# A two-block network on one NeuronCore: elementwise work moved from GpSimd to VectorE, two modulation vectors summed on TensorE strips, and one tile for the rotation tables

## The chip, the cores and the metric

The kernel runs on one core of a Trainium2 chip. The metric is the time of one execution in microseconds on the device, the median of three runs. The engines are called TensorE (PE in the profile; PEld is its loading of weights), VectorE (DVE), ScalarE (ACT), GpSimd (POOL) and SyncE (SP, which here only issues DMAs).

## The reference

Two transformer-like blocks run one after the other on 256 tokens of width 2048, all in float32. What matters of them:

```python
# first block: six vectors of 2048 from the condition c modulate its two norms and gate its two halves
mod = silu(c) @ w_ada + b_ada                                  # 2048 x 12288
shift1, scale1, gate1, shift2, scale2, gate2 = split(mod, 6)   # parts 0 to 5
p = modulate(rms_norm(x), shift1, scale1) @ w_in               # fourier mix and a two-way mLSTM
x = x + gate1 * (mix @ w_out)
h2 = modulate(rms_norm(x), shift2, scale2)                     # the second norm: parts 3 and 4
a, v = split(conv(h2 @ w_up))
x = x + gate2 * ((silu(a) * v) @ w_down)
# second block: a gated FFN, a mixer of a diagonal state-space model (S5) and a sparse attention (NSA), a gated FFN
h = h + 0.5 * norm(swiglu(norm(h)))
proj = norm(h) @ w_in_2
x_t = a * x_{t-1} + b * u_t        # S5: 64 groups x 64 complex states
h = h + norm((sig(ga) * y_ssm + sig(gb) * y_nsa) @ w_out_2)
h = h + 0.5 * norm(swiglu(norm(h)))
```

## The kernel before

Activations lie feature by feature: a tile holds 128 features x 256 tokens. Every matrix is packed into **chunks** of 128 x 1024 floats (512 KB). Each chunk is loaded by SP into a raw tile `wr` (four buffers; while the first mixer runs, every third goes to one of two buffers `wa`). ScalarE copies it to `wh` (rounded to fp32r, three buffers), and raw minus `wh` gives the rest `wl` (two buffers); that subtraction, the **low part**, is VectorE's, except that in some stages every `pool_every`-th chunk's is GpSimd's (method `chunk`). TensorE then does three products of each weight tile, `wh` with the high and low half of the activation and `wl` with the high half: 24 matmuls of 128 x 128 x 256 a chunk. All linears go through `lin_steps`; their evacuations come from PSUM (eight banks `ps`) at the end of a group of output tiles.

Beside a linear, generators run as **background**: after each chunk every one in `self.bg` is advanced at a rate of its own. These matter here:

- `ada_part` makes a part of `mod` (parts 2, 4, 3 during the first mixer, part 5 during the up projection after it). It loads the 32 chunks of the part's matrix, and VectorE adds each, scaled by a column of `silu_c`, to an accumulator `acc` (a scalar_tensor_tensor of 128 x 1024). Sixteen one-column matmuls then sum over the partitions. Parts 0 and 1 are made otherwise, in `entry`, at the start: two matmuls a chunk with a stationary operand of 32 columns, each into its own quarter of the partitions of a bank (a **strip**). There `sil`, 32 columns a weight row with `silu_c` in the first and zeros in the others, is the stationary operand, and the four strips are summed with a column of ones.
- `s5_tables`, during the second block's first up projection (`up2`), builds for each of 32 state tiles a cosine and a sine table by complex products (`cmul`, six elementwise operations on GpSimd), and writes them to DRAM (`d_tab`).
- `s5`, during the projections `kv_in2`, `q_in2`, `gn_in2` and `ga_in2`, takes a state tile per step: two products of the input with the tables on VectorE, an add and a subtract on GpSimd, two scans (tensor_tensor_scan) on VectorE, two more products on VectorE, an add and a subtract on GpSimd. All its tiles are called `w`.
- `nsa`, from `ga_in2` on, is the attention.

GpSimd also multiplies the two halves of the gated FFNs (`hidden`), adds the first twelve squares for each norm (`add_square`), adds the residuals in `post_norm`, and takes some products and sums in the mixers. One line of the profile, L277, is `tt` on VectorE; L280 is `gtt`, the same on GpSimd; L283 is scalar_tensor_tensor on VectorE; L274 is ScalarE; L295 is every matmul.

The instructions of each engine stand in the order that the framework's scheduler finds from its own model of times; an engine works through its queue in that order.

Of the kernel before, what the change touches and what calls it, by code (L numbers as in the profile page):

```python
# [226 lines left out]
class Builder:  # L227
    def __init__(self, tc, ap, out):
        self.tc = tc
        self.nc = tc.nc  # L230
        self.ap = ap
        self.out = out
        self.n = 0
        self.bg = []
        self.nchunk = 0
        self.nraw = 0
        self.more = None
        self.pool_every = 0
# [40 lines left out]
    def gtt(self, out, a, b, op):  # L279
        return self.nc.gpsimd.tensor_tensor(out, a, b, op=op)  # L280

# [23 lines left out]
    def chunk(self, src, n):  # L305
# [89 lines left out]
    def add_square(self, st, src, scale=None):  # L395
# [9 lines left out]
        if n < 12:  # L405
            self.gtt(st["acc"], st["acc"], s, ALU.add)
# [68 lines left out]

    def modulated(self, xs, st, gain, shift):
# [16 lines left out]
    def setup(self):  # L493
# [9 lines left out]
        self.ones_col = self.ones[:, 0:1]  # L503
        self.eps = self.small("eps", [P, 1])
# [5 lines left out]
    def block1(self):  # L510
# [3 lines left out]
        with tc.tile_pool(name="mix1", bufs=1, reuse_waits="tile") as pm:  # L514
# [24 lines left out]
            self.pool_every = 0  # L539
# [53 lines left out]
    def hidden(self, ph, a, b):  # L593

        m = self.t2()
        self.gtt(m, a, b, ALU.mult)
# [6 lines left out]
    def entry(self, pm, M, xs, h):  # L603
# [17 lines left out]
        self.pool_every = 3  # L621
        stream = self.lin_steps("qk_in", act_h, ev_qk)

        sil = self.new(pm, "vh", [P, 2, T], F32, 7).rearrange("p a (b c) -> p (a b) c", c=32)
        nc.gpsimd.memset(sil, 0.0)
        nc.vector.tensor_copy(sil[:, :, 0:1], self.silu_c.unsqueeze(2))
# [7 lines left out]
        def sums(kp, qt):  # L634
# [6 lines left out]
            for i in range(2):  # L641

                rt = qt * 2 + i
                g = rt % 4 * 32
                self.mm(acc[g:g + 32], sil[:, rt], raw[:, i * 512:(i + 1) * 512], rt < 4, rt >= KD - 4, True)

        def total(kp):
            acc = self.t2().rearrange("p a b -> p (a b)")
            self.act(acc, accs.pop(kp), ACT.Copy)
            for e in range(4):  # L650
                c = 4 * kp + e
                self.mm(mods[:, 0, c:c + 1], acc[:, e * P:(e + 1) * P], self.ones_col, e == 0, True, True)
# [38 lines left out]
        self.pool_every = 2  # L691
# [3 lines left out]
    def mix1(self, pm, M, h, qk, graw):  # L695
# [79 lines left out]
        def ev_o(gi, banks):  # L775
            for _ in ml:
                pass
            for b in range(2):
# [3 lines left out]
                self.gtt(o, o, hm[hd], ALU.mult)  # L782
# [12 lines left out]
    def mlstm(self, pm, qk, vfm, graw, hm):  # L795
# [102 lines left out]
        def values(hd, d):  # L898
# [15 lines left out]
            else:  # L914
                self.gtt(hx, hx, held.pop(("h", hd)), ALU.add)
# [193 lines left out]
    def cmul(self, out_r, out_i, ar, ai, br, bi, u, v):  # L1109

        self.gtt(u, ar, br, ALU.mult)
        self.gtt(v, ai, bi, ALU.mult)
        self.gtt(out_r, u, v, ALU.subtract)
        self.gtt(u, ar, bi, ALU.mult)
        self.gtt(v, ai, br, ALU.mult)
        self.gtt(out_i, u, v, ALU.add)
# [563 lines left out]
```

## Time and profile before

| | us |
|---|---|
| median of 3 runs | 3678.48 (3677.97 to 3678.49) |
| the profiled execution | 3664.88 |
| its span, first to last instruction | 3662.9 |
| PE busy in the span | 3540.0 (97%) |
| DVE busy | 2178.8 (59%) |
| ACT busy | 1557.1 (43%) |
| POOL busy | 891.9 (24%) |

The numbers are those of one profiled execution. Busy is the time in which at least one instruction of the engine ran; a share over the whole span mixes stages with different limits. The profiled execution took 13.6 us less than the median of the runs.

### The profile page before, as it was taken

What the parts mean: (1) busy time and instruction counts of PE and PEld (TensorE: products, weight loads), DVE (VectorE), ACT (ScalarE), POOL (GpSimd) and SP (SyncE); (2) the same over time, 40 slices, a digit from 0 to 9 for tenths busy, and PEclk for the clock granted to TensorE, in tenths of its full rate; (3) what the DMA queues carried; (4) which work ended last, traced back from release to release, by engine and by line L of the source; (5) the groups of instructions that cost most, each with busy time, mean ns of one, the idle gap of its engine ahead of it and who ended that gap; (6) DMA issues with size and microseconds to landing.
All of it is one profiled execution on the core that took longest, in us unless ns stands there. A gap on an engine that the chain in (4) does not pass through costs nothing. (4 is left out here: it accounts for less than half of the span.)

```text
span 3662.9 us, 67909 instructions
## 1 busy us (share of the span) xinstructions
PE 3540.0 (97%) x28008; PEld 3386.3 (92%) x28008; DVE 2178.8 (59%) x2597; ACT 1557.1 (43%) x1996; POOL 891.9 (24%) x799
## 2 busy tenths in 40 slices
PE   7899999999999999999999899999999899999998
PEld 4688899999999998999999888888899899999997
DVE  2487766666554665655544689775535655555445
ACT  2343355454544443444434423345544444444333
POOL 1143510000011059910000246433232300000001
PEclk9899999999999999999999999999999899999999
DMA  9887857776555566665556455444455455555554
GB/s 341 292 298 260 296 180 229 222 229 201 184 185 183 164 196 201 214 202 183 182 183 184 151 166 170 157 142 125 121 179 182 137 184 184 182 183 183 185 184 139
DMA packets 213319, 710.82 MB, mean 194 GB/s; under 512 B 23904, under 2 KB 39296, under 8 KB 213008
## 3 DMA queue, kind: packets, MB, share of 16 engines
q1 hardware_dynamic: 213008, 706.48, 60.0%
q8 instruction: 219, 3.59, 0.4%
q14 instruction: 92, 0.75, 0.1%
HBM read 694.29 MB, written 11.57 MB: 193 GB/s over the span
## 5 line engine op out<-in xcount | busy, mean ns | idle before, releaser
L277 DVE TENSOR_TENSOR wl<-wr,wh 128x1024 fp32r<-128x1024 f32 x989 | 1285.8, 1302 | 1074.0 <-PE ps L295 984.4
L274 ACT ACTIVATE wh<-wr 128x1024 fp32r<-128x1024 f32 x1066 | 1127.8, 1058 | 1594.9 <-PE ps L295 1390.4
L295 PE MATMUL ps<-r,wh 128*128 128x256 f32 x12224 | 1767.8, 287 | 38.9 <-ACT r L274 22.8
L295 PEld LDWEIGHTS ps<-r,wh 128*128 128x128 f32 x12224 | 1605.8, 194 | 65.3 <-ACT r L274 28.3
L295 PE MATMUL ps<-r,wl 128*128 128x256 f32 x6112 | 1012.4, 288 | 33.3 <-DVE wl L277 29.5
L295 PEld LDWEIGHTS ps<-r,wl 128*128 128x128 f32 x6112 | 856.8, 195 | 59.1 <-DVE wl L277 38.6
L280 POOL TENSOR_TENSOR t<-t,t 128x512 f32<-128x512 f32 x66 | 104.2, 1579 | 1290.2 <-ACT t L274 946.4
L295 PE MATMUL ps<-hh,wl 128*128 128x256 f32 x2112 | 345.4, 283 | 0.0
L295 PE MATMUL ps<-hl,wh 128*128 128x256 f32 x2112 | 345.4, 283 | 0.0
L295 PE MATMUL ps<-hh,wh 128*128 128x256 f32 x2112 | 344.3, 283 | 0.0
L295 PEld LDWEIGHTS ps<-hl,wh 128*128 128x128 f32 x2112 | 293.9, 192 | 0.0
L295 PEld LDWEIGHTS ps<-hh,wl 128*128 128x128 f32 x2112 | 293.9, 192 | 0.0
L280 POOL TENSOR_TENSOR wl<-wr,wh 128x1024 fp32r<-128x1024 f32 x77 | 196.8, 2556 | 396.3 <-PE ps L295 300.0
L295 PEld LDWEIGHTS ps<-hh,wh 128*128 128x128 f32 x2112 | 293.2, 192 | 0.0
L280 POOL TENSOR_TENSOR acc<-acc,t 128x256 f32<-128x256 f32 x99 | 109.6, 1115 | 607.6 <-ACT t L274 604.3
L283 DVE SCALAR_TENSOR_TENSOR acc<-wr,silu_c,acc 128x1024 f32<-128x1024 f32 x89 | 128.4, 1443 | 53.2 <-DMA wr<-in_w_ada 52.8
L280 POOL TENSOR_TENSOR w<-w,w 128x256 f32<-128x256 f32 x128 | 125.1, 1003 | 127.3 <-DVE w L277 120.1
L295 PE MATMUL ps<-m,wh 128*128 128x256 f32 x1024 | 152.3, 287 | 0.0
L280 POOL TENSOR_TENSOR t<-hh,hh 128x256 f32<-128x256 f32 (+4 forms) x192 | 149.5, 806 | 2.6
L295 PEld LDWEIGHTS ps<-m,wh 128*128 128x128 f32 x1024 | 134.6, 193 | 3.6 <-ACT wh L274 0.3
L277 DVE TENSOR_TENSOR w<-ps,w 128x512 f32<-128x512 f32 (+1 forms) x96 | 58.7, 640 | 50.8 <-DMA w<-d_rel 38.1
L277 DVE TENSOR_TENSOR hl<-t,hh 128x512 fp32r<-128x512 f32 x66 | 49.9, 756 | 65.2 <-ACT hh L274 65.2
(235 smaller groups left out, 2172.3 us busy)
## 6 DMA issues: line engine op xcount, KB each, us to landing
wr<-in_w_up SPq DMA_DIRECT2D x528, 512.0 KB, 4.0
wr<-in_w_down SPq DMA_DIRECT2D x264, 512.0 KB, 3.6
wr<-in_w_ada SPq DMA_DIRECT2D x139, 512.0 KB, 4.7
wa<-in_w_ada SPq DMA_DIRECT2D x53, 512.0 KB, 5.2
wr<-in_w_out SPq DMA_DIRECT2D x53, 512.0 KB, 3.7
wr<-in_w_ga_in SPq DMA_DIRECT2D x32, 512.0 KB, 3.6
wr<-in_w_glu SPq DMA_DIRECT2D x32, 512.0 KB, 3.6
wr<-in_w_gb_in SPq DMA_DIRECT2D x32, 512.0 KB, 3.6
```

The costliest lines, as they stand in the source:

```text
L274: return self.nc.scalar.activation(out=out, in_=in_, func=func, **kw)
L277: return self.nc.vector.tensor_tensor(out, a, b, op=op)
L280: return self.nc.gpsimd.tensor_tensor(out, a, b, op=op)
L283: return self.nc.vector.scalar_tensor_tensor(out=out, in0=a, scalar=s, in1=b, op0=op0, op1=op1)
L295: self.nc.tensor.matmul(out, lhsT, rhs, start=start, stop=stop, skip_group_check=skip)
```

## The change

1. `gtt`, the elementwise operation on GpSimd, is gone. All its uses become `tt` on VectorE: the low parts that `pool_every` gave to GpSimd, the squares, `hidden`, `cmul`, the residuals and the products in the mixers. GpSimd keeps memsets, the masks of the mLSTM, one sign change in `s5` and one add of two in the very last norm.
2. Parts 4 and 3 of `mod`, the second norm's, are made by a new `ada_strips`: two chunks per two steps, each in two matmuls of 32 columns x 512, so that the four fill the four strips of one bank. Parts 2 and 5 stay with `ada_part`. In `entry`, the stationary operand of the strips is now a column of `silu_c` read 32 times, and a column that picks one row a strip takes the place of the ones.
3. In `s5` the cosine and sine tables get a tile of three tables, `tab`, whose third is minus the sine (a copy on ScalarE), so that an add and a subtract of 128 x 256 each become one add of 128 x 512. The `w` tiles go from 12 to 11 buffers.

```diff
     def chunk(self, src, n):
...
         self.act(hi[:, 0:n], raw[:, 0:n], ACT.Copy)
-        self.nchunk += 1
-        tt = self.gtt if self.pool_every and self.nchunk % self.pool_every == 0 else self.tt
-        tt(lo[:, 0:n], raw[:, 0:n], hi[:, 0:n].bitcast(F32), ALU.subtract)
+        self.tt(lo[:, 0:n], raw[:, 0:n], hi[:, 0:n].bitcast(F32), ALU.subtract)
...
         if n < 12:
-            self.gtt(st["acc"], st["acc"], s, ALU.add)
+            self.tt(st["acc"], st["acc"], s, ALU.add)
             return
...
+    def strip_sum(self, bank, g, k, part, first, last):
+
+        sc = self.silu_c[:, k:k + 1].to_broadcast([P, 32])
+        self.mm(bank[32 * g:32 * g + 32], sc, part, first, last, True)
+
+    def ada_strips(self, part, dest):
+
+
+        w = self.ap["w_ada"]
+        ps = None
+        for half in range(2):
+            bank = self.ps().rearrange("p a b -> p (a b)")
+            for k in range(0, KD, 2):
+                raws = []
+                for kk in (k, k + 1):
+                    raw = self.raw()
+                    o = (((part - 2) * 2 + half) * KD + kk) * P * CH
+                    self.nc.sync.dma_start(raw, w[o:o + P * CH].rearrange("(p n) -> p n", p=P))
+                    raws.append(raw)
+                for i in range(4):
+                    kk, h = i // 2, i % 2
+                    self.strip_sum(bank, i, k + kk, raws[kk][:, h * 512:(h + 1) * 512], k == 0, k == KD - 2)
+                yield
+                yield
+            acc = self.t2().rearrange("p a b -> p (a b)")
+            self.act(acc, bank, ACT.Copy)
+            if ps is None:
+                ps = self.ps()
+            for n in range(8):
+                self.mm(ps[:, 0, half * 8 + n:half * 8 + n + 1], acc[:, n % 4 * P:(n % 4 + 1) * P],
+                        self.strips[:, n // 4:n // 4 + 1], True, True)
...
             def rest():
-                for part in (2, 4, 3):
-                    yield from self.ada_part(part, self.mod[:, part])
+                yield from self.ada_part(2, self.mod[:, 2])
+                for part in (4, 3):
+                    yield from self.ada_strips(part, self.mod[:, part])
...
         m = self.t2()
-        self.gtt(m, a, b, ALU.mult)
+        self.tt(m, a, b, ALU.mult)
...
         def load_tab(j):
-            tab = new(pm, "w", [P, 2, T], F32, 12)
-            nc.sync.dma_start(tab, self.d_tab[j])
+
+            tab = new(pm, "tab", [P, 3, T], F32, 2)
+            nc.sync.dma_start(tab[:, 0:2], self.d_tab[j])
+            self.act(tab[:, 2], tab[:, 1], ACT.Copy, scale=-1.0)
...
             self.tt(p, bu, cs, ALU.mult)
-            self.tt(r, sw(bu), sn, ALU.mult)
-            self.gtt(p[:, 0], p[:, 0], r[:, 0], ALU.add)
-            self.gtt(p[:, 1], p[:, 1], r[:, 1], ALU.subtract)
-            z = new(pm, "w", [P, 2, T], F32, 12)
+            self.tt(r, sw(bu), tab[:, 1:3], ALU.mult)
+            self.tt(p, p, r, ALU.add)
+            z = new(pm, "w", [P, 2, T], F32, 11)
...
             self.tt(x, z, cs, ALU.mult)
-            self.tt(r, sw(z), sn, ALU.mult)
-            self.gtt(x[:, 0], x[:, 0], r[:, 0], ALU.subtract)
-            self.gtt(x[:, 1], x[:, 1], r[:, 1], ALU.add)
+            self.tt(r, sw(z), tab[:, 2:0:-1], ALU.mult)
+            self.tt(x, x, r, ALU.add)
```

How this moves the queues is seen at three places. The first is TensorE's queue in the last products of `out1`, the first block's output projection; `x2` is two matmuls alike. Before, the products of one chunk (`wh_3777`, `wl_3778`) directly follow those of the chunk before it (`wh_3744`):

```order
L295 MATMUL ps_3608<-r_3254,wh_3744 128x256 x2
L295 MATMUL ps_3609<-r_3254,wh_3744 128x256 x2
L295 MATMUL ps_3608<-r_3260,wh_3777 128x256 x2
L295 MATMUL ps_3609<-r_3260,wh_3777 128x256 x2
L295 MATMUL ps_3608<-r_3260,wl_3778 128x256 x2
```

After, at the same chunks of the same projection:

```order
L290 MATMUL ps_3661<-r_3298,wh_3801 128x256 x2
L290 MATMUL ps_3662<-r_3298,wh_3801 128x256 x2
L290 MATMUL ps_3385<-wa_3829,silu_c_95 32x512 x2
L290 MATMUL ps_3385<-wr_3831,silu_c_95 32x512 x2
L290 MATMUL ps_3661<-r_3304,wh_3839 128x256 x2
L290 MATMUL ps_3662<-r_3304,wh_3839 128x256 x2
```

Four strips, those of two raw tiles, stand between two chunks. In the whole program the 64 pairs of strips of parts 4 and 3 stand in 36 such clusters, 28 of four matmuls and 8 of two.

The second is VectorE's queue during `up2`, while `s5_tables` runs; `wl` is a chunk's low part, `t` and `hh` are the tables' steps. Before:

```order
L277 TENSOR_TENSOR hl_15800<-t_2267_15797,hh_15799 128x512
L277 TENSOR_TENSOR wl_15908<-wr_15905,wh_15907 128x1024
L277 TENSOR_TENSOR wl_15938<-wr_15935,wh_15937 128x1024
L277 TENSOR_TENSOR wl_15978<-wr_15975,wh_15977 128x1024
L277 TENSOR_TENSOR wl_16008<-wr_16005,wh_16007 128x1024
```

After, at the same chunks:

```order
L275 TENSOR_TENSOR wl_16017<-wr_16014,wh_16016 128x1024
L275 TENSOR_TENSOR hh_16044<-t_2295_16045,t_2296_16046 128x256
L275 TENSOR_TENSOR hh_16114<-t_2304_16115,t_2305_16116 128x256
L275 TENSOR_TENSOR t_2321_16199<-hh_14494,hh_14698 128x256
L275 TENSOR_TENSOR t_2322_16200<-hh_14589,hh_14793 128x256
L275 TENSOR_TENSOR wl_16057<-wr_16054,wh_16056 128x1024
L275 TENSOR_TENSOR t_2330_16269<-hh_14494,hh_14698 128x256
L275 TENSOR_TENSOR t_2331_16270<-hh_14589,hh_14793 128x256
L275 TENSOR_TENSOR t_2339_16339<-hh_14494,hh_14698 128x256
L275 TENSOR_TENSOR t_2340_16340<-hh_14589,hh_14793 128x256
L275 TENSOR_TENSOR wl_16087<-wr_16084,wh_16086 128x1024
```

Four steps of the tables now stand between two low parts.

The third is VectorE's queue during `ga_in2`, while `s5` runs; the rows with `mag` are the scans, those from `ps` the first products. Before:

```order
L277 TENSOR_TENSOR wl_25409<-wr_25406,wh_25408 128x1024
L277 TENSOR_TENSOR w_25391<-ps_25388,w_25266 128x512
L277 TENSOR_TENSOR w_25392<-ps_25388,w_25266 128x512
L277 TENSOR_TENSOR wl_25427<-wr_25424,wh_25426 128x1024
L1386 SCALAR_TENSOR_TENSOR w_25397<-mag_13704,w_25391 128x256 x2
L277 TENSOR_TENSOR wl_25470<-wr_25467,wh_25469 128x1024
L277 TENSOR_TENSOR w_25400<-w_25397,w_25266 128x512
L277 TENSOR_TENSOR w_25401<-w_25397,w_25266 128x512
L277 TENSOR_TENSOR wl_25502<-wr_25499,wh_25501 128x1024
```

After, at the same four chunks and for the same state tile:

```order
L275 TENSOR_TENSOR wl_25466<-wr_25463,wh_25465 128x1024
L1409 SCALAR_TENSOR_TENSOR w_25336<-mag_13783,w_25331 128x256 x2
L275 TENSOR_TENSOR w_25339<-w_25336,tab_25222 128x512
L275 TENSOR_TENSOR w_25340<-w_25336,tab_25222 128x512
L275 TENSOR_TENSOR w_25450<-ps_25447,tab_25325 128x512
L275 TENSOR_TENSOR w_25451<-ps_25447,tab_25325 128x512
L275 TENSOR_TENSOR wl_25484<-wr_25481,wh_25483 128x1024
L275 TENSOR_TENSOR w_25339<-w_25339,w_25340 128x512
L275 TENSOR_TENSOR w_25450<-w_25450,w_25451 128x512
L275 TENSOR_TENSOR wl_25527<-wr_25524,wh_25526 128x1024
L1409 SCALAR_TENSOR_TENSOR w_25455<-mag_13783,w_25450 128x256 x2
L275 TENSOR_TENSOR wl_25559<-wr_25556,wh_25558 128x1024
```

The adds that GpSimd had (`w_25339`, `w_25450`) stand in VectorE's queue, and the state tiles are taken in a later phase.

## Rows read from the trace of the kernel before

**Rows 1.** Busy time by stretch: stretch, length, then each engine, clock, DMA share, GB/s.

```profile
core 0: us, PE busy (x) PEld busy (x) DVE busy (x) ACT busy (x) POOL busy (x), PEclk, DMA share, GB/s
...
235.00:447.00 212.00, 202.06 (x1557) 190.85 (x1556) 170.40 (x169) 82.15 (x132) 93.56 (x47) 0.98 0.82 282
...
1308.00:1573.00 265.00, 253.18 (x2065) 251.44 (x2064) 154.59 (x133) 103.86 (x108) 240.83 (x307) 0.98 0.62 205
...
2110.00:2430.00 320.00, 302.22 (x2144) 261.61 (x2142) 267.10 (x349) 108.73 (x130) 167.15 (x150) 0.96 0.51 163
...
2905.00:3640.00 735.00, 735.00 (x6128) 735.00 (x6127) 377.00 (x333) 301.44 (x313) 41.77 (x33) 1.00 0.58 181
```

**Rows 2.** Waits of PE from 235 to 447 us: total, times, longest.

```profile
PE ps L295 <- DVE wl L277: 8.3, 3, 4.1
```

**Rows 3.** The same from 1308 to 1573 us.

```profile
PE ps L295 <- DVE wl L277: 7.1, 6, 2.0
PE ps L295 <- ACT wh L274: 4.7, 1, 4.7
```

**Rows 4.** The same from 2110 to 2430 us.

```profile
PE ps L295 <- DVE wl L277: 9.1, 8, 2.5
PE ps L295 <- POOL w L280: 5.1, 3, 2.1
```

**Rows 5.** Timeline of PE in the entry, two strips (four records): start, length.

```profile
92.27 0.76 PE L295 MATMUL ps<-r,wh 128*128 128x256 f32 x5
92.95 1.05 PE L295 MATMUL ps<-wr,vh 128*32 128x512 f32 x4
93.94 0.39 PE L295 MATMUL ps<-r,wl 128*128 128x256 f32 x1
```

**Rows 6.** The same, four strips (eight records, two raw tiles).

```profile
95.23 0.88 PE L295 MATMUL ps<-r,wh 128*128 128x256 f32 x6
96.03 0.62 PE L295 MATMUL ps<-wr,vh 128*32 128x512 f32 x2
96.05 0.62 PE L295 MATMUL ps<-wa,vh 128*32 128x512 f32 x2
...
97.03 0.74 PE L295 MATMUL ps<-r,wh 128*128 128x256 f32 x4
```

**Rows 7.** Groups of VectorE, 235 to 447 us: count, busy, mean, idle before, releaser.

```profile
L283 DVE SCALAR_TENSOR_TENSOR acc<-wr,silu_c,acc 128x1024 f32<-128x1024 f32 x40 | 59.7, 1493 | 19.6 <-DMA wr<-in_w_ada 19.4
L283 DVE SCALAR_TENSOR_TENSOR acc<-wa,silu_c,acc 128x1024 f32<-128x1024 f32 x22 | 42.7, 1941 | 9.0 <-DMA wa<-in_w_ada 8.8
```

**Rows 8.** Tiles and lines of the whole span: duration in ns, minimum/median/maximum.

```profile
L277 DVE TENSOR_TENSOR wl<-wr,wh x989: 1149/1225/3364, 29.5 to 3636.5; 128x1024 fp32r<-128x1024 f32 x198
L277 DVE TENSOR_TENSOR sm<-sm,gates x32: 151/161/2224, 2449.5 to 2647.7; 128x2 f32<-128x2 f32 x32
L277 DVE TENSOR_TENSOR hh<-hh,hh x20: 415/422/537, 1296.1 to 1328.1; 128x256 f32<-128x256 f32 x20
L277 DVE TENSOR_TENSOR w<-w,w x64: 670/685/693, 2131.9 to 2432.6; 128x512 f32<-128x512 f32 x64
L1386 DVE TENSOR_TENSOR_SCAN w<-mag,w x64: 657/792/2810, 2129.0 to 2431.3; 128x256 f32<-128x256 f32 x64
L280 POOL TENSOR_TENSOR wl<-wr,wh x77: 2342/2402/3957, 65.4 to 2714.9; 128x1024 fp32r<-128x1024 f32 x77
```

**Rows 9.** Groups of VectorE and GpSimd, 1308 to 1573 us.

```profile
L277 DVE TENSOR_TENSOR wl<-wr,wh 128x1024 fp32r<-128x1024 f32 x86 | 125.0, 1462 | 72.0 <-PE ps L295 59.7 <-ACT wh L274 8.2 <-issue 2.5
...
L280 POOL TENSOR_TENSOR t<-hh,hh 128x256 f32<-128x256 f32 x128 | 119.4, 962 | 0.8
L280 POOL TENSOR_TENSOR hh<-t,t 128x256 f32<-128x256 f32 x64 | 61.5, 981 | 0.5
```

**Rows 10.** The same, 2110 to 2430 us.

```profile
L277 DVE TENSOR_TENSOR wl<-wr,wh 128x1024 fp32r<-128x1024 f32 x62 | 88.7, 1436 | 16.1 <-PE ps L295 12.0 <-issue 2.6 <-POOL w L280 1.3
L1386 DVE TENSOR_TENSOR_SCAN w<-mag,w 128x256 f32<-128x256 f32 x62 | 64.2, 1057 | 13.2 <-POOL w L280 13.1
...
L280 POOL TENSOR_TENSOR w<-w,w 128x256 f32<-128x256 f32 x125 | 122.9, 1008 | 124.7 <-DVE w L277 117.5 <-issue 7.2
L280 POOL TENSOR_TENSOR wl<-wr,wh 128x1024 fp32r<-128x1024 f32 x15 | 38.6, 2575 | 49.3 <-PE ps L295 38.9 <-issue 10.5
```

More of the change, by code (lines that the diff above doesn't have):

```diff
@@ L474, in ada_part @@
         yield
+    def strip_sum(self, bank, g, k, part, first, last):
[25 more added lines that the diff above has]
+                        self.strips[:, n // 4:n // 4 + 1], True, True)
+        o, _ = POFF["b_ada"]
+        self.tt(dest, ps[:, 0, 0:16], self.params[:, o + part * 16:o + part * 16 + 16], ALU.add)
+        yield
     def modulated(self, xs, st, gain, shift):
@@ L503, in setup @@
         self.ones_col = self.ones[:, 0:1]
+        self.strips = self.small("strips", [P, 3])
+        nc.gpsimd.memset(self.strips, 0.0)
+        for g in range(4):
+            nc.gpsimd.memset(self.strips[32 * g:32 * g + 1, g % 2:g % 2 + 1], 1.0)
+            nc.gpsimd.memset(self.strips[32 * g:32 * g + 1, 2:3], 1.0)
         self.eps = self.small("eps", [P, 1])
@@ L643, in sums @@
                 rt = qt * 2 + i
-                g = rt % 4 * 32
-                self.mm(acc[g:g + 32], sil[:, rt], raw[:, i * 512:(i + 1) * 512], rt < 4, rt >= KD - 4, True)
+                self.strip_sum(acc, rt % 4, rt, raw[:, i * 512:(i + 1) * 512], rt < 4, rt >= KD - 4)
         def total(kp):
@@ L651, in total @@
                 c = 4 * kp + e
-                self.mm(mods[:, 0, c:c + 1], acc[:, e * P:(e + 1) * P], self.ones_col, e == 0, True, True)
+                self.mm(mods[:, 0, c:c + 1], acc[:, e * P:(e + 1) * P], self.strips[:, 2:3], e == 0, True, True)
         def modulate(kp):
@@ L781, in ev_o @@
                 self.act(o, banks[b], ACT.Sigmoid)
-                self.gtt(o, o, hm[hd], ALU.mult)
+                self.tt(o, o, hm[hd], ALU.mult)
                 for i in range(2):
@@ L914, in values @@
             else:
-                self.gtt(hx, hx, held.pop(("h", hd)), ALU.add)
+                self.tt(hx, hx, held.pop(("h", hd)), ALU.add)
                 hm.append(hx)
@@ L1109, in cmul @@
     def cmul(self, out_r, out_i, ar, ai, br, bi, u, v):
[L1111 to L1116, printed above, removed]
+        self.tt(u, ar, br, ALU.mult)
+        self.tt(v, ai, bi, ALU.mult)
+        self.tt(out_r, u, v, ALU.subtract)
+        self.tt(u, ar, bi, ALU.mult)
+        self.tt(v, ai, br, ALU.mult)
+        self.tt(out_i, u, v, ALU.add)
     def ffn(self, up, down, h, act, rstd, post, next_gain, last=False, extra=None):
@@ L1386, in inputs @@
                 nc.vector.tensor_tensor_scan(z[:, k], mg, p[:, k], 0.0, op0=ALU.mult, op1=ALU.add)
-            x, r = new(pm, "w", [P, 2, T], F32, 12), new(pm, "w", [P, 2, T], F32, 12)
+            x, r = new(pm, "w", [P, 2, T], F32, 11), new(pm, "w", [P, 2, T], F32, 11)
             self.tt(x, z, cs, ALU.mult)
-            self.tt(r, sw(z), sn, ALU.mult)
-            self.gtt(x[:, 0], x[:, 0], r[:, 0], ALU.subtract)
-            self.gtt(x[:, 1], x[:, 1], r[:, 1], ALU.add)
+            self.tt(r, sw(z), tab[:, 2:0:-1], ALU.mult)
+            self.tt(x, x, r, ALU.add)
             tiles["x", j] = x
@@ L1566, in scores @@
             if br == 0:
-                bias = new(pm, "w", [P, 3, P], F32, 12)
+                bias = new(pm, "w", [P, 3, P], F32, 11)
                 nc.sync.dma_start(bias[:, 0], self.hankel(hi, P))
@@ L1576, in scores @@
             self.mm(ps[:, 2], q[m][ds, 0:P], k[ds, 0:P], True, True, True)
-            s = new(pm, "w", [P, 3, P], F32, 12)
+            s = new(pm, "w", [P, 3, P], F32, 11)
             self.tt(s.rearrange("p a b -> p (a b)"), ps[:, 0:3].rearrange("p a b -> p (a b)"),
@@ L1600, in turn @@
                 nc.tensor.transpose(tp[:, b], s[:, src], self.eye)
-            pt = new(pm, "w", [P, 3, P], F32, 12)
+            pt = new(pm, "w", [P, 3, P], F32, 11)
             self.act(pt, tp[:, 0:3], ACT.Copy)
```

27 lines of the change are left out of this document (6 added, 21 removed).

## The prediction

> **What bounds the kernel now.** I read the busy time by stretch first, then the waits of TensorE in the stretches where it is not full, then the groups of the engines that it waits for there. In the long up and down projections TensorE is simply full: 6128 matmuls in 735 us, or 0.120 us each, with no gap [rows 1]. A chunk of 24 matmuls takes 2.88 us there, and nothing off TensorE counts. Three stretches differ. In the first mixer, 235 to 447 us, TensorE is busy for 202 of 212 us and VectorE for 170; VectorE also waits 29 us for matrix chunks of `w_ada` to land [rows 1, 7], so both engines are nearly used up. While the tables are built, 1308 to 1573 us, GpSimd is busy for 241 of 265 us and TensorE loses a dozen [rows 1, 3]. While the state tiles are worked on, 2110 to 2430 us, VectorE is busy for 267 of 320 us, and TensorE waits for low parts and for GpSimd's adds [rows 1, 4]. The granted clock of these stretches is 0.98, 0.98 and 0.96 of the full one, which is the level of 1.2 GHz for a small part of the time. The change takes work from the engines with the short queues and gives some of it to TensorE, which has none to spare; so I ask what the strips cost there, and whether VectorE can do its own work and GpSimd's without making TensorE wait longer.
>
> **The strips, on the path.** The entry already has such strips, so their price can be read. Two strips: the last five ordinary matmuls start at 92.27 and use up 5 x 0.120 us, so the next could start at 92.87; the next ordinary matmul starts at 93.94, 1.07 us later [rows 5]. Four strips side by side: 95.23 + 6 x 0.120 = 95.95, the next at 97.03, 1.08 us later [rows 6]. So four cost what two cost, and the number of clusters counts: 28 x 1.08 + 8 x 1.07 = **38.8 us** of TensorE. The clusters stand between main chunks in the first mixer and `out1`, where TensorE is full but for 10 us [rows 1]. The final one-column sums are as many as before.
>
> What goes is 64 accumulations on VectorE, about 62 of them in this stretch (102 us there, [rows 7]). That frees VectorE far beyond need: 170 - 102 + 47, GpSimd's 94 us there [rows 1] at half (a low part takes 1.225 us on VectorE and 2.40 on GpSimd, [rows 8]), is 115 us of some 245. TensorE's waits for low parts, 8.3 us [rows 2], should mostly go: **-8 us**, between 0 and -8.3.
>
> The chunks of `w_ada` are loaded in the same number and size, but two at a time, and a raw buffer is now given back by TensorE, in its order, and not by VectorE. Behind a strip whose chunk has not landed stand all main products; behind a waiting accumulation stood only VectorE's queue. The nearest row is VectorE's 28.6 us of waits for these chunks [rows 7]. The bounds are 0 and 28.6; the stretch becomes some 30 us longer for the same bytes, and its buffers for main chunks come back earlier, so I take **+6 us**.
>
> **GpSimd's work on VectorE.** An operation alone takes 0.42 us for 256 columns on VectorE, 0.685 for 512 and 1.225 for 1024 [rows 8]; GpSimd takes 1.0 and 2.6 for the first and last [rows 9, 10]. And VectorE pays for GpSimd's company: the same low part takes between 1.15 and 3.36 us, and a two-column product that takes 0.16 us took up to 2.22, nearly one long instruction of GpSimd [rows 8]. While the tables are built a low part takes 1.462 us in the mean, so 86 x 0.237 = 20 us were lost [rows 9].
>
> Tables: VectorE's 155 us, less these 20, plus 192 operations x 0.42 = 81, plus the 60 us of GpSimd's smaller groups at the same ratio (0.42 to 0.97), 26, makes 242 of 265 us, 2.81 us a chunk (86 chunks) against TensorE's 2.88. It fits, barely. Between two low parts stand four steps, 4 x 0.42 + 1.225 = 2.9 us, now and then more; two `wl` buffers give a lead of about one chunk. Of the 11.8 us that TensorE waits now [rows 3], 4.7 were for a copy behind GpSimd's queue and go; new bursts give some back. **-5 us**, between -12 (all goes) and +12: the longest usual run between two low parts is a 512-wide and five 256-wide operations, 0.685 + 5 x 0.42 + 1.225 = 4.0 us, 1.1 over a chunk, once in each of 11 groups of output tiles.
>
> State tiles: 267 us, less 62 x 0.40 for the scans (1.057 against 0.657) and 62 x 0.21 for the low parts, plus 15 low parts x 1.225 and 64 adds x 0.685 [rows 8, 10], makes 267 - 25 - 13 + 18 + 44 = 291 of 320 us. VectorE does no less than before, but the way to GpSimd and back (13 us of waits before scans [rows 10], 5.1 us on TensorE [rows 4]) is gone. **-5 us**, between -14 (the 9.1 and 5.1 us of [rows 4]) and +20 (none of the lost 38 us comes back, 329, and 11 of VectorE's present 53 idle us stay). The extra copy on ScalarE is hidden: it is busy for 109 of 320 us [rows 1].
>
> The remaining places are small. In the two `post_norm` stretches VectorE gets 16 adds and 11 squares, 27 x 0.42 = 11 us, and loses as much of its lengthened instructions: **+3** for both, between -5 and +11. In the entry GpSimd's low parts of 2.4 us become 1.2 us behind a stage that waits for DMA: **-2**. In the up and down projections the added products lie beside a full TensorE: nothing.
>
> Sum: 38.8 - 8 + 6 - 5 - 5 + 3 - 2 = +27.8 us. The profiled execution took 3664.9, so 3692.7; the median of the runs lies 13.6 us above it, so **3706 us**, +0.75%. A measurement of this kernel can tell about 0.2%, 7.3 us, from no change.
>
> **The rivals.**
>
> *The released lock pays for all (faster).* Without GpSimd beside it VectorE is never held up, so it delivers on time everywhere. Then TensorE gets back its waits of [rows 2 to 4], 34.3 us, and the half clock that follows waits, 0.02 x 212 + 0.02 x 265 + 0.04 x 320 = 22.3 us [rows 1]: 38.8 - 56.6 = -18 us, 3661 as a median. It decides once more than 46 of the 57 us come back. For it speak the long low parts and two-column products above; against it, that the work that held VectorE up is now VectorE's own. The Trainium skill, "SBUF — State Buffer", section "Who interferes with whom", gives the rule behind it: a VectorE instruction with two SBUF inputs and a GpSimd instruction that reads SBUF shut each other out for the whole instruction. The maximum of 3.36 us, 1.2 of its own and 2.1 more, agrees with that.
>
> *It comes out even.* Half of that returns (28 us), and the strips lie half in the 10 us in which TensorE is not busy: 38.8 - 5 - 28 = +6 us, 3684. The rows speak against it as far as the waits for low parts in the first mixer are only 8.3 us.
>
> *VectorE becomes the bound of the tables and the state tiles.* Both upper bounds hold, +12 and +20 in place of -5 and -5: 42 us more, 3748 at most; halfway, 3727. The two sums of 242 of 265 and 291 of 320 speak for it, the two-chunk lead against.
>
> *Strips wait for their chunks.* 28.6 us in place of 6: 3729. For it speaks that DMA moves 282 GB/s there with a share of 0.82 [rows 1]; against it, that the demand per microsecond falls.
>
> **How the numbers follow.** The forecast 0.45 (alone 3690 to 3722, its small terms at half their bounds), VectorE the bound 0.17, strips waiting 0.13, even 0.13, faster 0.12. Slower by over 0.2% is the forecast with the two worse cases, 0.75; within 0.2% is the even case, 0.13; faster is 0.12. The range runs from 3672, where the even case begins, to 3744, short of the worst of the slow ones: 3672 to 3744.
>
> **What would show it.** In the profile after: TensorE's matmuls of 32 columns by 512 grow by 256 records, and in the first mixer about 39 us pass in clusters of 1.07 us each; the stretch that ends `out1` ends some 35 us later. VectorE's low part is 1.22 us in the mean, with no long ones; scans 0.66. GpSimd is idle but for masks. The tables' stretch shows VectorE at 0.9 or more. I am wrong if TensorE waits for `w_ada` by more than 10 us after the entry, if the tables or the state tiles grow by more than 10 us, or if more than 20 us come back there.

## The result: faster by 1.1%

The changed kernel takes 3638.5 us in the median (3634.6 to 3638.9, four runs) against 3678.5 of the kernel before (3678.0 to 3683.5 in the same comparison): ratio 0.9886, 95% interval 0.9869 to 0.9903. The forecast was 3706. The profiled execution of after took 3634.6 us, 3.9 below its median; that of before lay 13.6 below its own. So the traces differ by 30 us and the medians by 40, and I profiled the kernel before twice more to see where the missing 10 us lie ("before, again" below).

The whole of after, first part of its page: busy time, share of the span, instructions.

```profile
PE 3554.9 (98%) x28264; PEld 3372.4 (93%) x28264; DVE 2220.6 (61%) x3210; ACT 1580.4 (44%) x2033; POOL 20.0 (1%) x65
```

Busy time of after by stretch, columns as in [rows 1]: the first mixer with `out1`, the tables, the first `post_norm`, the state tiles.

```profile
202.00:485.00 283.00, 283.00 (x2142) 236.73 (x2141) 135.00 (x180) 103.37 (x161) 2.26 (x8) 0.99 0.73 255
1322.00:1570.00 248.00, 248.00 (x2070) 248.00 (x2069) 213.23 (x434) 104.11 (x108) 0.00 (x0) 1.00 0.69 220
2047.00:2095.00 48.00, 38.37 (x289) 36.74 (x290) 39.12 (x76) 25.77 (x47) 1.06 (x2) 0.93 0.45 141
2095.00:2414.00 319.00, 307.18 (x2213) 268.98 (x2212) 282.15 (x430) 124.41 (x161) 4.82 (x10) 0.97 0.53 167
```

TensorE does not stop once in the first mixer or the tables, where [rows 1] show 10 and 12 us without work. To compare stretches of different kernels I cut them at the first DMA issue of a stream: `u_in`, the first chunk of `up1`, the first store of `b_t`, the last table store, the first table load, `kv`, `glu`, `w_o`, the last chunk of `w_up`. "No strips" is the first experiment. Lengths in us:

| stretch ends at | before | again | again | after | no strips |
|---|---|---|---|---|---|
| `u_in` (entry) | 210.8 | 204.2 | 212.7 | 202.4 | 203.1 |
| `up1` (first mixer, `out1`) | 259.2 | 267.9 | 265.1 | 282.6 | 245.8 |
| `b_t` store | 838.5 | 839.5 | 838.8 | 836.7 | 837.7 |
| last table store | 264.4 | 274.7 | 276.3 | 247.8 | 246.2 |
| first table load | 476.8 | 476.8 | 476.8 | 477.5 | 477.9 |
| `kv` (`post_norm`) | 53.8 | 53.8 | 53.6 | 47.8 | 47.8 |
| `glu` (state tiles) | 333.9 | 332.4 | 332.0 | 318.6 | 316.8 |
| `w_o` | 269.8 | 270.2 | 270.5 | 272.1 | 273.6 |
| last `w_up` (`post_norm`) | 665.5 | 664.3 | 664.2 | 657.6 | 657.6 |
| end | 290.1 | 290.1 | 290.1 | 289.7 | 289.7 |

The first mixer, with the strips, is 15 to 23 us longer. What became shorter: the tables by 17 to 28, the state tiles by 13 to 15, the two `post_norm` stretches by 6 and 7 to 8, the entry by 2 to 10. The stretch that ends at `w_o` is 2 us longer.

The strips themselves cost what was forecast. TensorE in after, two strips (four records, as in [rows 5]) between ordinary matmuls (start, length):

```profile
385.07 0.75 PE L290 MATMUL ps<-r,wh 128*128 128x256 f32 x4
385.74 1.05 PE L290 MATMUL ps<-wr,silu_c 128*32 128x512 f32 x4
386.73 0.50 PE L290 MATMUL ps<-r,wl 128*128 128x256 f32 x2
```

From the strips' start to the next matmul pass 0.98 us; in the 28 clusters of four strips it is 0.995. By the prediction's way of counting, from 385.07 + 4 x 0.120 = 385.55, it is 1.18 us; but the first of those four matmuls itself follows a cluster (384.5) and takes longer than 0.120. So 36 clusters cost 36 to 42 us, and the first mixer without strips is 36.8 us shorter than in after.

### The profile page after: what moved, and what is told of

It reads as the page before. It is cut to its first block, busy times and chain, and to the rows that moved or that the text cites. A ratio compares the mean times of both kernels' runs of the same rounds, so it can differ in the third digit from the quotient of the medians.

```text
span 3632.8 us, 67934 instructions
## 1 busy us (share of the span) xinstructions
PE 3554.9 (98%) x28264; PEld 3372.4 (93%) x28264; DVE 2220.6 (61%) x3210; ACT 1580.4 (44%) x2033; POOL 20.0 (1%) x65
## 4 chain that ended last, share of the span: by engine, by line
PE 94%; DVE 3%; DMA 1%; ACT 1%; issue 1%; SPq 0%; ACTq 0%; DVEq 0%
PE ps L290 93%; DVE wl L275 1%; DVE r L278 1%; DVE t L275 0%; PE ps L1622 0%; DMA wr<-in_w_qk_in 0%; DVE w L275 0%; DMA r<-in_xT 0%; DMA wr<-in_w_ada 0%; ACT wh L272 0%; DVE r L275 0%; DMA tab<-d_tab 0%; DVE t L278 0%; DMA wa<-in_w_qk_in 0%; DMA wa<-in_w_ada 0%
## 5 line engine op out<-in xcount | busy, mean ns | idle before, releaser
L275 DVE TENSOR_TENSOR wl<-wr,wh 128x1024 fp32r<-128x1024 f32 x1064 | 1300.6, 1223 | 1105.7 <-PE ps L290 869.4
L290 PE MATMUL ps<-r,wl 128*128 128x256 f32 x6112 | 998.4, 285 | 9.0 <-DVE wl L275 8.9
L290 PE MATMUL ps<-wr,silu_c 128*32 128x512 f32 x348 | 78.6, 618 | 9.2 <-DMA wr<-in_w_ada 9.2
L278 DVE SCALAR_TENSOR_TENSOR acc<-wr,silu_c,acc 128x1024 f32<-128x1024 f32 x50 | 64.1, 1283 | 36.3 <-DMA wr<-in_w_ada 36.1
L290 PE MATMUL ps<-m,wl 128*128 128x256 f32 x512 | 83.0, 284 | 0.0
L278 DVE SCALAR_TENSOR_TENSOR t<-ps,params,t 128x255 f32<-128x255 f32 x176 | 76.6, 475 | 0.6
L272 ACT ACTIVATE t<-ps 128x256 f32<-128x256 f32 (+2 forms) x87 | 39.4, 458 | 85.2 <-PE ps L290 65.3
L275 DVE TENSOR_TENSOR wl<-wa,wh 128x1024 fp32r<-128x1024 f32 (+1 forms) x34 | 40.8, 1199 | 58.0 <-ACT wh L272 30.0
L290 PEld LDWEIGHTS ps<-m,wl 128*128 128x128 f32 x512 | 70.4, 191 | 3.9 <-DVE wl L275 1.7
L272 ACT ACTIVATE t<-ps,params 128x256 f32<-128x256 f32 x88 | 46.6, 563 | 55.5 <-PE ps L290 34.7
```

Of the source, the lines that this page charges most:

```text
L272: return self.nc.scalar.activation(out=out, in_=in_, func=func, **kw)
L275: return self.nc.vector.tensor_tensor(out, a, b, op=op)
L278: return self.nc.vector.scalar_tensor_tensor(out=out, in0=a, scalar=s, in1=b, op0=op0, op1=op1)
L290: self.nc.tensor.matmul(out, lhsT, rhs, start=start, stop=stop, skip_group_check=skip)
```

## The experiments

Each starts from the changed kernel (median 3638.5 us) unless it says otherwise. The experiments were measured in several comparisons; the median of before in them goes from 3672.3 to 3681.7 us, so a difference of some 5 us between two medians says little by itself, and the lengths of the stretches say more. Two theories of the gain were set against each other. **Company** (theory 1, or the lock, in the expectations): GpSimd, when it reads SBUF, lengthens VectorE's two-input instructions. **Queue** (theory 2): what stands on GpSimd's slow queue is late, and ScalarE, VectorE and TensorE wait behind it in their own order.

**The strips undone**, and the strips alone.

```diff
-yield from self.ada_part(2, self.mod[:, 2])
-for part in (4, 3):
-    yield from self.ada_strips(part, self.mod[:, part])
+for part in (2, 4, 3):
+    yield from self.ada_part(part, self.mod[:, part])
```

> The changed kernel with the modulation's parts 4 and 3 accumulated on VectorE again (128 chunks of w_ada in all its places, no strips outside the entry); all else as changed. Theory 1 (the strips are a plain loss, hidden by what GpSimd's removal gives): the 36 clusters of 0.98 to 1.00 us leave TensorE, 36 us, and VectorE, busy for 135 of 283 us in that stretch, takes 64 accumulations of 1.27 us = 81 us without making TensorE wait by more than 12 us: 3602 to 3615 us, and the stretch from u_in's first load to up1's first load falls from 283 to some 247 to 259. Rival (the strips pay for themselves by freeing VectorE): TensorE's waits of 12 us and the half clock come back and more, 3630 to 3640 us.

Measured: 3598.6 us, 0.9797 (0.9768 to 0.9827) of before, 39.9 less than after; its first mixer 245.8 us. That is theory 1 of the strips, and a little more than it: they are a plain loss, and without them the rest of the change is worth 80 us (3678.9 to 3598.6).

The kernel before with these lines the other way round, so with strips and all of GpSimd's work:

> The kernel before with one part of the change: parts 4 and 3 of the modulation by strips; all GpSimd work stays. The prediction's terms for it alone: 38.8 of TensorE, 8 of waits back, 6 of new waits: +36.8, so 3710 to 3720. Theory 1 of the strips (a plain loss of 36 us of TensorE, less the 13 us that the stretch from u_in to up1 loses to waits in the kernel before, 259.2 against 245.8 us without strips and without GpSimd): +23 to +26, 3698 to 3706, the stretch at 282 to 287 us.

Measured: 3696.7 us, 1.0045 (1.0028 to 1.0063) of before, +17; the first mixer 282.6 us as in after. Less than either expectation: the stretch costs TensorE 36 us more, and it had been losing 13 to 22 us there, not the 8 of [rows 2].

**The tables' products on GpSimd again** (`self.tt` to `self.gtt`, GpSimd's `tensor_tensor`, in `cmul`).

> The changed kernel with the 256-column and smaller products of the rotation tables (cmul, 288 operations) on GpSimd again; all else as changed. Both theories of GpSimd (its company lengthens VectorE's instructions; its own queue is what TensorE waits for) expect the loss of that stretch back: 16.7 us, 3651 to 3656. Rival (prediction's step: tables worth 5 us, the rest came from other parts of the change): 3641 to 3645.

Measured: 3643.5 us (3636.0 to 3644.2), and the stretch of the tables did not grow: 246.4 us. Both theories failed as stated. The median rose by 5.0 us, and by the traces most of it lies elsewhere: the state tiles take 326.8 us against 318.6, and 3.5 come back up to `w_o`. The code there is the same; the order of the instructions in the queues is not, and what the order alone costs was not tried. One group of VectorE and a wait of TensorE in that stretch:

```profile
L275 DVE TENSOR_TENSOR wl<-wr,wh 128x1024 fp32r<-128x1024 f32 x86 | 126.5, 1475 | 70.5 <-PE ps L293 64.4 <-ACT t L272 2.7 <-issue 2.1
```
```profile
PE ps L293 <- DVE wl L275: 0.6, 1, 0.6
```

The low part is as slow as in [rows 9], 1475 against 1462 ns, and TensorE waits 0.6 us: company is there, but VectorE has 167 us of work in 247 and can afford it. So something else on GpSimd made the loss.

**The tables and the hidden product** of the feed-forwards on GpSimd.

```diff
 def hidden(self, ph, a, b):
     m = self.t2()
-    self.tt(m, a, b, ALU.mult)
+    self.gtt(m, a, b, ALU.mult)
```

> The changed kernel with the rotation tables' products and also the feed-forward's hidden products (44 of 512 columns in up2, as many in each other up projection) on GpSimd again. With the tables alone on GpSimd the stretch from the first b_t store to the last table store took 246.4 us and TensorE lost nothing, against 264.4 in the kernel before. Theory 2 (GpSimd's queue: a hidden product stands behind up to six table products, and ScalarE's copy, VectorE's subtraction and then the chunk's copies stand behind it): that stretch goes to 260 to 266 us, the whole to 3650 to 3660. Theory 1 (only the lengthening of VectorE's instructions counts): the lengthening was there with the tables alone and did no harm; the stretch stays at 246 to 250, the whole at 3638 to 3648.

Measured: 3669.0 us, the stretch 277.3: more than the queue theory expected. And the reverse, the kernel before with the hidden product alone on VectorE:

> The kernel before with one line changed: the hidden product of the feed-forwards on VectorE; tables, low parts, sums and adds stay on GpSimd. Theory 2 (that product stands behind table products on GpSimd's queue, ScalarE's copy and VectorE's subtraction behind it): the stretch from the first b_t store to the last table store falls from 264.4 to 246 to 250 us, the whole to 3645 to 3664. Theory 1 (the company of the table products, which stays): the stretch at 260 or more, the whole at 3672 to 3682.

Measured: 3650.4 us, 0.9914 (0.9896 to 0.9932) of before; the stretch 244.4. One line gives 31 us. The chain could be read in the trace of before. ScalarE's waits, then VectorE's, 1308 to 1573 us (total, times, longest):

```profile
ACT hh L274 <- POOL t L280: 23.7, 8, 10.6
```
```profile
DVE hl L277 <- ACT hh L274: 35.4, 10, 8.3
```

and VectorE's in the kernel with the one line changed, 1305 to 1560 us:

```profile
DVE hl L277 <- ACT hh L274: 7.3, 10, 0.8
```

The product stands behind table products, for up to 10.6 us, as long as ten of them take. ScalarE's copy `hh` waits for it, VectorE's `hl` for that, and the chunk copies and low parts behind both come late. In the kernel with the one line changed TensorE waits for nothing in that stretch.

The queue is only a part of the 31 us. The same `hl` in before's first profile (1364 to 1384 us) and in its second (1366 to 1400 us; start, length, what it waited for), and TensorE's wait in the second, 1311.6 to 1586.3 us:

```profile
1377.29 1.12 DVE L277 TENSOR_TENSOR hl<-t,hh 128x512 fp32r<-128x512 f32 x1 [8.33 <-ACT hh L274]
```
```profile
1380.56 14.99 DVE L277 TENSOR_TENSOR hl<-t,hh 128x512 fp32r<-128x512 f32 x1 [8.92 <-ACT hh L274]
```
```profile
PE ps L295 <- DVE wl L277: 18.9, 6, 14.0
```

In the second profile VectorE's subtraction of two tiles of SBUF took 15.0 us in place of 1.1, while GpSimd ran 24 table products without a gap, and TensorE stood for 14.0 us behind the low part after it. That looks like company in its worst form. It is there in four of the five executions that have both the table products and the hidden product on GpSimd (before's second and third, before with strips, after with both on GpSimd; not before's first), and in none of the three kernels that have the table products there without the hidden product: their longest `hl` takes 1.2 us. So 10 to 12 us of the 31, by which the stretch is shorter in the first profile of before than in the other two, go with one hold-up of VectorE, and the rest with the queue. Why it strikes this one instruction is not shown.

**GpSimd busy, and nobody waiting for it.** Beside the tables on VectorE, six products of a tile of ones for each table, or twelve memsets:

```diff
+    for _ in range(6):
+        nc.gpsimd.tensor_tensor(dum[:, 1], dum[:, 0], dum[:, 0], op=ALU.mult)
```
```diff
+    for _ in range(12):
+        nc.gpsimd.memset(dum, 1.0)
```

> The changed kernel and, beside the tables on VectorE, 192 GpSimd products of 256 columns that read a tile of ones and write one that nobody reads: no instruction waits for them. Theory 1 (GpSimd's company is the cost): VectorE's low part rises from 1.22 to about 1.45 us in that stretch, and as VectorE now has 213 us of work there, TensorE waits 10 us or more: 3649 us or above. Theory 2 (only the way through GpSimd's queue cost): VectorE's times and the whole stay, 3636 to 3641.

> The same, with GpSimd busy at 384 memsets of 512 columns (0.53 us each, about 200 us), which read nothing of SBUF. Theory 1 in the form that reading is what shuts VectorE out: no change, 3636 to 3641, low part 1.22 us. Theory 1 in the form that any work of GpSimd's on SBUF does it: as with the products, 3649 or above. Theory 2: no change.

Measured: 3677.6 us with the products, 3639.7 with the memsets, as the company theory in its reading form had it. The products ran in one go from 1230 to 1410 us, partly before the first `b_t` store; the stretches on its two sides grew by 20 and 18 us. VectorE there (1245 to 1412), and TensorE's wait (1240 to 1412):

```profile
L275 DVE TENSOR_TENSOR wl<-wr,wh 128x1024 fp32r<-128x1024 f32 x41 | 60.2, 1469 | 16.2 <-PE ps L290 16.2
L275 DVE TENSOR_TENSOR hh<-hh,hh 128x256 f32<-128x256 f32 x20 | 14.9, 771 | 2.2 <-DMA hh<-in_b_re 2.0 <-DMA hh<-in_b_im 0.2
...
L275 DVE TENSOR_TENSOR t<-ps,rstd 128x512 f32<-128x512 f32 x6 | 4.0, 679 | 0.0
```
```profile
PE ps L290 <- DVE wl L275: 28.8, 18, 7.5
```

VectorE and GpSimd beside memsets, 1327 to 1575 us:

```profile
L275 DVE TENSOR_TENSOR wl<-wr,wh 128x1024 fp32r<-128x1024 f32 x86 | 105.3, 1224 | 31.9 <-issue 17.6 <-PE ps L290 9.2 <-ACT hh L272 2.5
...
L1136 POOL MEMSET dum<- 128x512 f32 x217 | 114.2, 526 | 12.5
```

So company is real where VectorE has no time to spare, and only with a GpSimd that reads: 1469 ns beside products, 1224 beside memsets, and a product with one input in PSUM keeps its 679. By that the trace agrees with the Trainium skill, "SBUF — State Buffer", section "Who interferes with whom": a VectorE instruction with two SBUF inputs contends with a GpSimd instruction that reads SBUF, not with one that only writes it, as a memset does, and with at most one SBUF input it does not contend (the page excepts VectorE's two-port modes).

**The state tiles' adds on GpSimd again**, with their tables as before; **the low parts** on GpSimd again (the `pool_every` lines restored); and both.

```diff
-    tab = new(pm, "tab", [P, 3, T], F32, 2)
-    nc.sync.dma_start(tab[:, 0:2], self.d_tab[j])
-    self.act(tab[:, 2], tab[:, 1], ACT.Copy, scale=-1.0)
+    tab = new(pm, "w", [P, 2, T], F32, 12)
+    nc.sync.dma_start(tab, self.d_tab[j])
...
-    self.tt(p, p, r, ALU.add)
+    self.gtt(p[:, 0], p[:, 0], r[:, 0], ALU.add)
+    self.gtt(p[:, 1], p[:, 1], r[:, 1], ALU.subtract)
```

> The changed kernel with the state tiles as before: 128 adds of 256 columns on GpSimd, tables in two parts without the negated copy; all else as changed. Theory 1 and theory 2 alike, as the adds are on the chain and their company lengthens the scans: the stretch from kv's first load to glu's first load goes from 318.6 to 328 to 334 us, the whole to 3646 to 3655. Rival (the 15 low parts on GpSimd made the loss there): within 3 us of the changed kernel, 3636 to 3642.

> The changed kernel with every second, third or fifth low part of the mixers on GpSimd again (93 of them, 2.4 to 2.6 us each in place of 1.22). Theory 2 (TensorE waits for the low part that takes 2.5 us and stands in another queue): the entry gets its 8 us back, the state tiles some 5, 3648 to 3655. Rival (a lead of two chunks covers 2.5 us): 3636 to 3643.

> The changed kernel with the state tiles' adds and the low parts both on GpSimd again (apart they gave -9.5 and +10 us). Theory 2 (two kinds of work on one queue wait behind each other: an add behind a low part of 2.4 us, with VectorE's scan and TensorE behind it): the stretch from kv's first load to w_o's first load, 590.7 us as changed, 586.5 and 592.7 with the one and with the other, goes to 599 to 606, the whole to 3648 to 3655. Additive: the stretch at 588 to 590, the whole at 3637 to 3641.

Measured: 3629.0 us with the adds on GpSimd, *faster* than after by 9.5; 3648.6 with the low parts (+10.1); 3654.3 with both (+15.9, where adding them up gives +0.7). The stretch from `kv` to `w_o` is 586.6, 592.6 and 602.5 us (590.7 in after). Each kind of work alone is nearly carried; together they are not. The state tiles with the adds alone on GpSimd, then with both (first TensorE's waits in the two kernels, then VectorE's scans in the two):

```profile
PE ps L293 <- POOL w L278: 1.5, 1, 1.5
PE ps L293 <- DVE wl L275: 1.0, 2, 0.6
```
```profile
PE ps L295 <- DVE wl L277: 11.0, 9, 3.9
PE ps L295 <- POOL w L280: 5.0, 3, 2.1
```
```profile
L1412 DVE TENSOR_TENSOR_SCAN w<-mag,w 128x256 f32<-128x256 f32 x64 | 51.7, 833 | 9.2 <-POOL w L278 9.2
```
```profile
L1422 DVE TENSOR_TENSOR_SCAN w<-mag,w 128x256 f32<-128x256 f32 x64 | 66.5, 1061 | 13.2 <-POOL w L280 13.1
```

The queue theory forecast the size, but the rows do not show that it is the cause. VectorE waits only 3.9 us longer for the adds, of which in only four of 64 pairs the first begins directly behind a low part. The scans, 228 ns longer in the mean beside low parts of 2.6 us, and the low parts on VectorE that TensorE waits for, speak for company. Both are at work; how much each costs was not separated.

**The copy or the adds?** After, 2095 to 2413 us, waits of TensorE and of ScalarE; then ScalarE and TensorE in the first `post_norm` stretch, 2047 to 2095 us:

```profile
PE ps L290 <- DVE w L275: 7.1, 2, 3.8
```
```profile
ACT tab L272 <- DMA tab<-d_tab: 46.0, 24, 6.4
```
```profile
ACT tab L272 <- DMA tab<-d_tab: 4.4, 2, 4.1
```
```profile
PE ps L290 <- ACT r L272: 6.8, 2, 6.2
```

The new copy on ScalarE stands in front of other copies and waits for a table that only two buffers let load early. To part the copy from the adds: tables as before, four adds of 256 columns on VectorE.

> The changed kernel with the rotation tables of the state tiles loaded as before (two parts in a tile of the ring of 12, no copy on ScalarE), and the adds on VectorE, but as four of 256 columns in place of two of 512. VectorE gets 32 x (4 x 0.42 - 2 x 0.685) = 10 us more, ScalarE 13 us less and none of the 50 us that it stands before the copy waiting for the table to land. Theory 3 (in the state tiles the changed kernel loses by that copy, which holds up ScalarE's chunk copies): 3627 to 3632. Rival (it loses because the adds are on VectorE): 3637 to 3645.

Measured: 3634.3 us (3633.6 to 3635.9), between the two and 4 us from after, which the medians hardly tell apart. By stretch theory 3 fell where it was made for: the state tiles take 318.6 us with the copy and without, so ScalarE's 46 us of waiting there cost nothing. What the copy costs lies in the `post_norm` stretch, 47.8 against 45.3 us, where the first table's copy stands 4.1 us in front of `r`. The adds' share is in `kv` to `w_o`: 587 to 588 us in the three kernels with the adds on GpSimd and all low parts there on VectorE, 589 to 596 in the ten with the adds on VectorE too. As these ten differ by 7 us with nearly the same code there, the share has a sign but no size.

**Sums of squares and the post norms' adds on GpSimd again** (`self.tt` to `self.gtt` in `add_square` and `one`).

> The changed kernel with the sums of squares (99 adds of 256 columns) and the post norms' adds (28) on GpSimd again. Theory: the two stretches around the post norms give back what they gained, 6 and 8 us, and out1's end nothing: 3650 to 3654. Rival (the prediction's: VectorE loses as much by the work as it gains, 0 to 3 us): 3636 to 3643.

Measured: 3649.6 us, +11.1; the two stretches 55.9 and 664.6 us, +8.1 and +7.0. Two groups of that kernel's first such stretch, 2049 to 2105 us:

```profile
L275 DVE TENSOR_TENSOR t<-r,rstd 128x256 f32<-128x256 f32 x16 | 11.5, 755 | 0.1
```
```profile
L278 POOL TENSOR_TENSOR r<-r,t 128x256 f32<-128x256 f32 x14 | 13.1, 954 | 3.0 <-DVE t L275 3.0
```

Slowness and company meet: the adds are a link of the chain, 954 ns each where VectorE takes 420, and VectorE's own link beside them takes 755 in place of 420. TensorE has little else to do; its granted clock is 0.79 there and 0.93 in after.

**The first mixer without strips.** With every second low part there on GpSimd, then with products on GpSimd that nobody needs in their places:

```diff
+    self.nchunk += 1
+    if self.pool_every and self.nchunk % self.pool_every == 0:
+        self.nc.gpsimd.tensor_tensor(self.dum, self.ones, hi[:, 0:P].bitcast(F32), op=ALU.mult)
+        for _ in range(3):
+            self.nc.gpsimd.tensor_tensor(self.dum, self.ones, self.eye, op=ALU.mult)
```

> The changed kernel without strips (3598.6 us), with every second low part of the first mixer on GpSimd again. Both theories: the stretch from u_in's first load to up1's first load goes from 245.8 to 258 to 268 us and the whole to 3610 to 3622; if neither holds, 246 to 250 and 3596 to 3603.

> The changed kernel without strips, all low parts on VectorE, and at every second chunk of the first mixer four GpSimd products of 128 columns on tiles that nobody needs (some 2.6 us together, as long as a low part on GpSimd). Theory 1 (GpSimd's company lengthens VectorE's instructions, which are 206 us of 246 there): the accumulations go from 1.28 to 1.45 us or more, the stretch to 256 us or more. Theory 2 (only the way through GpSimd's queue): accumulations at 1.28 to 1.32, the stretch at 245 to 249 us.

Measured: 3617.1 us, the stretch 261.9; and 3606.7, the stretch 251.4. VectorE's accumulations there, without GpSimd (no strips), with low parts, with unneeded products:

```profile
L278 DVE SCALAR_TENSOR_TENSOR acc<-wr,silu_c,acc 128x1024 f32<-128x1024 f32 x46 | 58.8, 1279 | 12.9 <-DMA wr<-in_w_ada 12.7
```
```profile
L283 DVE SCALAR_TENSOR_TENSOR acc<-wr,silu_c,acc 128x1024 f32<-128x1024 f32 x46 | 74.2, 1612 | 20.2 <-DMA wr<-in_w_ada 20.0
```
```profile
L280 DVE SCALAR_TENSOR_TENSOR acc<-wr,silu_c,acc 128x1024 f32<-128x1024 f32 x46 | 61.2, 1331 | 10.3 <-DMA wr<-in_w_ada 10.1
```

The first expectation held; of the second, neither theory did. Short products lengthen an accumulation by 52 ns and cost 5.6 us; long low parts lengthen it by 333 ns and the stretch grows by 16. The short products were not quite without a waiter: one in four reads `wh`, and ScalarE's next copy waited for it four times, 6.2 us in all. With the low parts TensorE's waits there end on VectorE's low part for 8.3 us and on GpSimd's for 1.1, which speaks for company over queue here; but a long GpSimd instruction without a waiter was not tried, so the split stays open. With the strips, where VectorE has time to spare (busy for 135 of 283 us in after), the low parts on GpSimd cost this stretch nothing: 282.5 us.

**Before, again.** The unchanged kernel, profiled twice more.

> The kernel before, unchanged, profiled again. If the 13.6 us between its first profile and its median lie in the tables' stretch, then an execution near 3678 shows 272 to 280 us there in place of 264.4, and the other stretches within 2 us of the first profile; the rival is that they are spread over the entry and the mixers.

> The same once more: the stretch of the tables moves with the total time, the others by 2 us or less.

Measured: 3676.0 and 3682.1 us; lengths in the table above. The first profile is shorter by 10 and 12 us in the tables, where the other two have the `hl` of 15 us, and by 9 and 6 in the first mixer; the entry moves by -7 and +2. So half of the expectation held. Behind the tables, all three agree within 2 us in every stretch.

**What the two losses undone give:** no strips and the adds on GpSimd; then the table products on GpSimd as well.

> The changed kernel without the strips and with the state tiles' adds on GpSimd: the two parts that were a loss are undone, -39.9 and -9.5 us. They lie in different stretches, so they should add up: 3586 to 3593.

> The faster version of before (no strips, state tiles' adds on GpSimd) with the table products on GpSimd too. Queue theory: nothing stands behind them there, VectorE has idle time, so no change, 3590 to 3597. Lock theory: low part 1.47 us in that stretch and TensorE waits, 3600 or more.

Measured: 3593.6 us, 0.9768 (0.9753 to 0.9783) of before; and 3591.6, 0.9755 (0.9740 to 0.9769). The first is just outside its expectation: on top of the missing strips the adds give back 5.0 us, not 9.5, so the two do not quite add up. The second held: the tables can stay on GpSimd once nothing that others need stands behind them.

## Why the prediction was wrong

**The strips (+38.8) held** within 3 us, at 36 clusters of 0.98 to 1.00 us, and TensorE's records of 32 columns grew by 256. **New waits for `w_ada` (+6) did not come:** behind the entry TensorE has none. **Waits returned (-8) was too small:** -13 to -22 by the table (245.8 against 259 to 268). The net term, +36.8, is +17 measured on the kernel before.

**The step that failed is "It fits, barely ... -5 us" for the tables**, and with it the whole price of GpSimd's work. For everything but the strips I forecast about -9 beside the -8; it was -80 (3678.9 to 3598.6). In the tables alone one line, the hidden product moved to VectorE, gave 31 us in place of 5. By stretch, the three profiles of before against no strips, in the order of size: tables -18 to -30, first mixer -13 to -22, state tiles -15 to -17, `post_norm` -6 and -7 to -8, entry -1 to -10; the stretch to `w_o` is 3 to 4 longer.

- *Tables.* I took TensorE's 11.8 us of [rows 3] as the most there was to gain and let bursts on VectorE eat half. The bursts did no harm: VectorE was busy for 213 of 248 us, 0.86 where the sum had 242 of 265, and TensorE waited for no low part. And the 11.8 us were too few, for two reasons: they left out the granted clock, 0.98 in that stretch and 1.00 in after (5 us, a sum that the prediction made only for its rival), and they come from the one execution of three in which `hl` was not held up; in the others TensorE waits 24.0 and 24.7 us. The two rows that show where the queue's loss begins, ScalarE 23.7 us behind GpSimd and VectorE 35.4 us behind ScalarE, I did not read; I stopped at TensorE's own waits and put 4.7 us of them on that queue.
- *State tiles (-5).* -13 to -15 by the traces, because adds and low parts are no longer together on GpSimd (332.4 us with both there again, 318.0 and 322.5 with one), not from relief of VectorE, which is busy for 282 us against 276 before. Of queue and company there, the share of each stays open. The edit itself, adds on VectorE and the table in one tile, cost 5 to 9.5 us. "The extra copy on ScalarE is hidden" holds in the state tiles and fails for the first table, in the `post_norm` stretch.
- *`post_norm` (+3)* was -13. I weighed 11 us of added work on VectorE against its lengthened instructions, and these did cancel (busy for 42.6 us in the first stretch before, 39.1 after); left out was that the place is a chain, in which each add became shorter, 0.95 to 0.42 us, and VectorE's own link with it.
- *Entry (-2)* was -2 to -10; with the low parts back on GpSimd it is 6.6 us longer than after. Its three lengths before differ by 8 us, and why is not shown.

The rival "the released lock pays for all" had the right sign. Its point of decision, 46 of 57 us, was passed, as 80 came back; but the lock is only a part of it. In the tables the ordinary company stayed in the kernel with the one line changed (a low part takes 1395 ns there, 1462 in [rows 9]), and the loss went: it was the queue and the one hold-up of 15 us. In after, low parts on VectorE are 1223 ns in the mean and no longer than 1311, scans 668 in the median, as foreseen:

```profile
L275 DVE TENSOR_TENSOR wl<-wr,wh x1064: 957/1224/1311, 30.1 to 3606.6; 128x1024 fp32r<-128x1024 f32 x178
```

## What to carry to other kernels

When an engine waits, follow the chain through every in-order queue, not one step: the bottleneck's own waits show where the loss ends, the waits of the engines before it show where it begins and how much could come back. A slow engine may carry one kind of work that nobody needs soon, as GpSimd could the table products here; as soon as something that others wait for is queued behind it, try that one instruction elsewhere before moving the rest. Before pricing a stretch, look at a second execution of it, and there at the longest instruction of each kind: one `hl` of 15 us among eleven made most of the difference between two executions of the same kernel.

## What the runs showed that I had not expected

Each of the two engines can hold up the other for many instructions. VectorE stood for 15.0 us beside 24 GpSimd products of some 0.6 us each. GpSimd beside VectorE is held up in its turn: in the first mixer with unneeded products one of 128 columns, 0.45 us at its shortest, took 6.98 us: it stood beside six VectorE instructions in a row with two inputs from SBUF, and ended when one with an input from PSUM came. And busy time of GpSimd does not tell what VectorE loses: 131 us of short products, four at a time, cost an accumulation 52 ns in the mean; 87 us with long low parts cost it 333. Products of 256 columns without a pause, beside the tables, cost a low part 245. Where the low parts left GpSimd, VectorE did their work in about the time that it no longer lost: it is busy for 200 us in the first mixer of before's second profile, and for 206 without GpSimd and without strips.
